# One hybrid decoder block on one core: where the HGRN mixer turns its keys and makes its states, how its scores share banks, and where the first attention maxima stand

## The chip, the cores and the metric

The kernel is one launch on 1 of the cores of a Trainium2 chip. The metric is the device time in microseconds (us) of that core. Before the change it is 3009.27 us, the median of 3 runs (3007.25 to 3016.14). The engines are named as in the profile: PE (TensorE, the matrix products), DVE (VectorE), ACT (ScalarE), POOL (GpSimd) and SP (SyncE, which issues most of the DMAs, one after the other).

## The reference: what is computed

One decoder block over a sequence of 2048 tokens of width 1024, in float32. One input projection feeds two mixers: HGRN2, a gated linear recurrence with 4 heads of 128, and a dilated attention with 8 heads of 64 and three branches (window, dilation) = (128,1), (512,4), (2048,16). An output projection and a SwiGLU follow, each with its norm, shift, scale, gate and residual.

```python
h = modulate(rms_norm(x, norm1_g[l]), shift1, scale1)
hq, hf, hi, hgt, aq, ak, av = jnp.split(h @ w_in[l], split_at, axis=-1)
...
def step(state, inp):                      # one chunk of the recurrence
    q_c, k_c, v_c, b_c = inp
    o_inter = jnp.einsum('bhtk,bhkv->bhtv', q_c * jnp.exp(b_c), state)
    ...
    scores = jnp.einsum('bhtk,bhsk,bhtsk->bhts', q_c, k_c, decay)
    o_intra = jnp.einsum('bhts,bhsv->bhtv', scores, v_c)
    k_dec = k_c * jnp.exp(b_last[:, :, None, :] - b_c)
    state = jnp.exp(b_last)[..., None] * state + jnp.einsum('bhsk,bhsv->bhkv', k_dec, v_c)
...
s_max = jnp.max(s, axis=-1, keepdims=True)  # attention: the maximum of each row of scores
p = jnp.exp(s - s_max)
```

## The kernel before

The tokens are taken in four pieces of 512 (`c` = 0 to 3); two pieces are a half. In each half the input projection makes all its columns tile by tile: a tile of `feature_major` is one block of 128 columns for 512 tokens, 24 matmuls of 128x512 (8 blocks of the depth, three products each, because every operand is split into a high and a low part; L565 to L567, or L463 to L465 for `token_major`). Their weights are loaded as `wraw`, rounded to `whi` on ACT (L87) and brought to the rest `wlo` on POOL (L80). A tile ends in `psA` (four banks of PSUM) and is moved out by ACT and DVE. PSUM has eight banks: four for `psA`, two for `psM`, one for `psL` and one for `psO`.

The HGRN mixer `hg_mix` is a generator that runs beside these projections. One run of it, called a unit here, is one head and one piece of 512 tokens (four chunks of 128); there are 16 units. A unit makes its gates with three exponentials and logarithms over 128x1536 on ACT (`he`), a running sum `hb` on DVE, and decayed keys `hkd`. Then, on PE:
- K, the keys turned: four transposes of `hkd` into `psM` (L620), copied by ACT to `hkt` (L622);
- U, the state products `u` = `hkt` times values into `psM` (L657); DVE makes the four new states `hst` from it (L666);
- seven levels of scores, s0 to s6. A level's operands `hz` are made by POOL (two differences `hd`), ACT (one exponential, L644) and DVE (two products); s0 has its own (`hzq`, and the `hz<-hk,hd` product). Each is four matmuls (L677) into `psL`, which DVE then copies under a mask into `hsc` (L682). `level(n)` makes the operands of level n; `level(n + 2)` follows the copy of level n;
- the outputs, into `psO` (L693, L694); the sum of their squares, called ss here (L701); and `hy`, which DVE makes from `psO` and writes to HBM as `hg_d`.

The generator's `yield`s cut a unit into steps. `Beside` hands out the steps: `begin(work, matmuls, steps, credit)` starts a list of units, and each time that `matmuls / steps` projection matmuls have been issued, one step follows; `finish` runs what is left. `UNIT` is 16, and two units are planned as 33 steps over 240 matmuls, 288 or 192. On PE the order is as written here (`manual_schedule`). On the other engines a scheduler of the compiler sets the order from the dependencies and its own estimate of times, once, when the program is built.

After the last unit `first_maxima` closes the pool of the mixer and opens that of the attention: `open_attention` issues loads of constants, queries and keys of head 0 (`qs`, `kh`), further operands (`qx`, `kl`) and values. Then `maxima_steps` makes the scores of 48 blocks two by two on PE (L133), and DVE takes their row maxima (L141), beside the last projection tiles `att_qk(1, 3)`. `combine` turns the maxima (L147), sends parts of them through HBM (`m_d`, `mr`, `mn_d`) and puts them into a row of `qx`. The attention follows: L896 and L898 are its scores, L856 its values, and the maxima of the next head run beside it into `psS`.

Of the kernel before, what the change touches and what calls it, by code (L numbers as in the profile page):

```python
# [11 lines left out]
F32 = mybir.dt.float32  # L12
# [38 lines left out]
def hybrid_block(ctx, tc, xT, small, cst, w_ada, w_ft, w_tk, w_out, w_gu, w_dn, out):  # L51
# [286 lines left out]
    with ExitStack() as ab:  # L338
# [129 lines left out]
        with tc.tile_pool(name="ada0", bufs=2) as pl:  # L468
            xs0 = []
            for k in range(KT):  # L470
                xs0.append(pl.tile([P, CH], F32, name=f"x0_{k}", bufs=1))
                nc.sync.dma_start(out=xs0[k], in_=xT[:, k, 0:CH])
            x_stats(0, xs0)
            h_tiles(0)
            ps0 = [pp.tile([P, CH], F32, name="psA", tag="psA", bufs=4) for _ in range(4)]
            tags = itertools.cycle(("psM", "psL"))

            def psum():
                tag = next(tags)
                return pp.tile([P, CH], F32, name=tag, tag=tag, bufs=2 if tag == "psM" else 1)  # L480

            LAG0 = 1

            bg = pl.tile([P, 8], F32, name="bg", bufs=1)
            dve.scalar_tensor_tensor(bg, sm[:, V_B + 8:V_B + 16], 1.0, sm[:, V_G1:V_G1 + 8], ALU.add, ALU.mult)
            sums, ws0 = {}, {}
            with tc.manual_schedule(engines={mybir.EngineType.PE}):
              done = {}
              for k in range(KT + LAG0):
                  if k < KT:  # L490
                      sums[k] = ada_sums(pl, cact, (k, 8 + k), 4, psum, 2)
                      if k % 2 == 0:
                          ws0[k] = ws0[k + 1] = split_w(wp, w_tk[0, k // 2])
                  if 0 < k <= KT:
                      n = k - 1
                      act.activation(mods[:, n:k], sums[n][:, 0:1], AF.Identity, bias=sm[:, V_B + n:V_B + k])
                      act.activation(gs1[:, n:k], sums[n][:, 1:2], AF.Identity, scale=sm[:, V_G1 + n:V_G1 + k],
                                     bias=bg[:, n:k])
                      with tc.issue_after(done[n - 2]) if n > 1 else nullcontext():
                          done[n] = h_apply(0, n, xs0[n])  # L500
                  if k >= LAG0:
                      token_major_k(0, k - LAG0, ps0, *ws0[k - LAG0])
# [90 lines left out]
        def hg_mix(hd, c, x):  # L593
# [21 lines left out]
            yield  # L615
            yield
            yield
            kt_ps = pp.tile([P, CH], F32, name="psM", tag="psM", bufs=2)
            for n in range(4):
                pe.transpose(kt_ps[:, n * P:(n + 1) * P], kd[:, n * P:(n + 1) * P], ident)  # L620
            kt = T("hkt")
            act.copy(kt, kt_ps)  # L622

            sc = T("hsc")
            lr = T("hd", 2)
# [20 lines left out]
                tt(dve, w(z)[:, :, 1, :], w(dd)[:, :, 1, :], w(q)[:, :, 1, :], ALU.mult)  # L646

            level(1)
            yield

            v = v_of[c]
            vn = [v[:, n, hd * P:(hd + 1) * P] for n in range(4)]
            ns = range(3 if c == NCH - 1 else 4)
            u = pp.tile([P, CH], F32, name="psM", tag="psM", bufs=2)
            for n in ns:
                ts = slice(n * P, (n + 1) * P)
                pe.matmul(u[:, ts], kt[:, ts], vn[n], start=n == 0, stop=n == ns[-1], skip_group_check=True)  # L657
            before = [states[hd]]
            for n in ns:
                ts = slice(n * P, (n + 1) * P)  # L660
                new = hw.tile([P, P], F32, name="hst", tag=f"hst{hd}", bufs=2) if n == 3 else \
                    hw.tile([P, P], F32, name="hst", tag="hst", bufs=3)
                if before[-1] is None:
                    dve.tensor_copy(new, u[:, ts])
                else:
                    dve.scalar_tensor_tensor(new, before[-1], eb[:, n * P + 127:n * P + 128], u[:, ts],  # L666
                                             ALU.mult, ALU.add)
                before.append(new)
            if len(ns) == 4:
                states[hd] = before[4]  # L670
            for lv in range(7):
                yield
                zk, zq = zs.pop(lv)
                ps = pp.tile([P, CH], F32, name="psL", tag="psL", bufs=1)
                for n in range(4):
                    ts = slice(n * P, (n + 1) * P)
                    pe.matmul(ps[:, ts], zk[:, ts], zq[:, ts], start=n == 0, stop=n == 3, skip_group_check=True)  # L677
                m = cs[:, C_MASK + lv * P:C_MASK + (lv + 1) * P].unsqueeze(1)
                if lv == 0:
                    tt(dve, c4(sc), c4(ps), m.broadcast_to([P, 4, P]), ALU.mult)  # L680
                else:
                    dve.copy_predicated(c4(sc), m.bitcast(U32).broadcast_to([P, 4, P]), c4(ps))  # L682
                if lv < 5:
                    level(lv + 2)
                elif lv == 5:
                    tt(dve, q, q, eb, ALU.mult)
            yield
            yield
            o_ps = pp.tile([P, CH], F32, name="psO", tag="psO", bufs=1)
            for n in range(4):  # L690
                ts = slice(n * P, (n + 1) * P)
                if before[n] is not None:
# [18 lines left out]
        def units(hd, xs):  # L711
            return [hg_mix(hd, c, x) for c, x in xs.items()]
# [42 lines left out]
        def second_half():  # L755
            token_major(1, 0)
            xs = hg_project(1, 0)
            for hd, others in ((1, lambda: att_qk(1, 0)), (2, lambda: token_major(1, 1, (2,))),
                               (3, lambda: token_major(1, 1, (3,)))):
                beside.begin(units(hd - 1, xs), 240, 2 * UNIT + 1)  # L760
                xs = hg_project(1, hd)
                others()
            beside.begin(units(3, xs), 192, 2 * UNIT + 1)
            att_qk(1, 1)
            att_qk(1, 2)
            beside.finish()

        first_psum = []

        def first_maxima():  # L770

            tags = itertools.cycle(("psL", "psO", "psM", "psM"))

            def psum():
                tag = next(tags)
                return pp.tile([P, CH], F32, name=tag, tag=tag, bufs=2 if tag == "psM" else 1)
            first_psum.append(psum)

            hwx.close()
            open_attention()  # L780
            beside.begin([maxima(0, psum)], 96 - 36, 24, -36)

        with tc.manual_schedule(engines={mybir.EngineType.PE}):
            make_h(1)
            first_half()
            make_h(2)
            make_h(3)
            second_half()
            first_maxima()
            att_qk(1, 3)  # L790
            beside.finish()
        combine(0, first_psum[0])
        dve.scalar_tensor_tensor(gs2, mods[:, 32:40], 1.0, sm[:, V_G2:V_G2 + 8], ALU.add, ALU.mult)


# [613 lines left out]
```

## Time and profile before

| what | value |
|---|---|
| median of 3 runs | 3009.27 us (3007.25 to 3016.14) |
| the profiled execution | 3006.01 us, span 3004.2 us |
| PE busy | 2829.4 us (94% of the span) |
| DVE, ACT, POOL busy | 68%, 44%, 47% |
| mean granted TensorE clock | 0.979 |

The units run from about 130 to 495 us (first half) and from 570 to 899 us (second half); the first maxima and the start of the attention lie between 899 and 966 us. After about 1215 us come the output projection and the SwiGLU. A view of the profile gives for each engine what it did and, in square brackets, how long it stood idle before an instruction and what ended that wait. The granted clock has two levels here, 1.0 (2.4 GHz) and 0.5 (1.2 GHz); a number between is a mean over a stretch.

### The profile page before, as it was taken

How to read it: one execution, taken by the hardware profiler on the slowest of the kernel's cores; microseconds unless marked ns; L12 is line 12 of the kernel's file. 1: busy time of each engine (PE TensorE's matmuls, PEld its weight loads, DVE VectorE, ACT ScalarE, POOL GpSimd, SP SyncE). 2: the span in 40 equal slices, each digit the busy share in tenths (PEclk: the TensorE clock that was granted, in tenths of full speed). 3: DMA queues.
4: the chain of work that ended last, by engine and by line, in shares of the span. 5: the costliest groups of instructions: out<-in, count | busy, mean ns of one | idle time of the engine just before them, and what ended most of it. 6: DMA issues, size and time to landing. Idle time of an engine off the chain costs nothing. (4 is left out here: it accounts for less than half of the span.)

```text
span 3004.2 us, 45023 instructions
## 1 busy us (share of the span) xinstructions
PE 2829.4 (94%) x16308; PEld 2601.9 (87%) x16308; DVE 2041.7 (68%) x3781; ACT 1313.2 (44%) x2392; POOL 1404.8 (47%) x1076
## 2 busy tenths in 40 slices
PE   6899999999997999999999999999999998999998
PEld 4777777787776999997778999999999998999998
DVE  7677756355554565677777676688677669776676
ACT  4533445344331665666554333345333335443334
POOL 5333443434332232320045666557566655665664
PEclk9999999999997999999999999999999999999999
DMA  6422335111138474537843222123242222232221
GB/s 245 151 99 103 111 141 180 62 64 69 55 116 210 120 164 104 134 109 251 294 158 130 82 73 85 64 78 108 83 133 74 81 71 93 85 114 65 84 75 66
DMA packets 212319, 344.37 MB, mean 115 GB/s; under 512 B 24816, under 2 KB 97392, under 8 KB 209008
## 3 DMA queue, kind: packets, MB, share of 16 engines
q1 hardware_dynamic: 202272, 323.40, 34.9%
q10 hardware_dynamic: 9824, 18.09, 1.6%
q8 instruction: 128, 2.10, 0.3%
q14 instruction: 95, 0.78, 0.1%
HBM read 282.44 MB, written 58.98 MB: 114 GB/s over the span
## 5 line engine op out<-in xcount | busy, mean ns | idle before, releaser
L80 POOL TENSOR_TENSOR wlo<-wraw,whi 128x512 fp32r<-128x512 f32 (+1 forms) x542 | 850.0, 1589 | 480.5 <-ACT whi L87 222.1
L1003 PE MATMUL psG<-chi,whi 128*128 128x344 f32 (+1 forms) x1848 | 596.4, 323 | 20.8 <-DVE hm L80 14.1
L1005 PE MATMUL psG<-chi,wlo 128*128 128x344 f32 (+1 forms) x1848 | 591.9, 320 | 1.5 <-POOL wlo L80 1.5
L1004 PE MATMUL psG<-clo,whi 128*128 128x344 f32 (+1 forms) x1848 | 593.2, 321 | 0.0
L274 ACT CAST whi<-wraw 128x512 fp32r<-128x512 f32 x520 | 311.0, 618 | 403.9 <-issue 191.6
L1003 PEld LDWEIGHTS psG<-chi,whi 128*128 128x128 f32 x1848 | 350.3, 190 | 26.5 <-DVE hm L80 9.3
L1265 PE MATMUL psD<-ahi,whi 128*128 128x344 f32 (+1 forms) x1056 | 346.5, 328 | 20.2 <-DVE xc L1268 19.7
L1268 DVE SCALAR_TENSOR_TENSOR xc<-psD,mods,xc 128x344 f32<-128x344 f32 (+1 forms) x528 | 290.2, 568 | 91.8 <-PE psD L1267 91.5
L1005 PEld LDWEIGHTS psG<-chi,wlo 128*128 128x128 f32 x1848 | 349.3, 189 | 2.7 <-POOL wlo L80 2.7
L1004 PEld LDWEIGHTS psG<-clo,whi 128*128 128x128 f32 x1848 | 349.1, 189 | 0.3 <-issue 0.2
L80 POOL TENSOR_TENSOR wlo<-wt,whi 128x512 fp32r<-128x512 f32 x132 | 192.6, 1469 | 314.6 <-ACT whi L274 238.3
L1267 PE MATMUL psD<-ahi,wlo 128*128 128x344 f32 (+1 forms) x1056 | 338.0, 320 | 0.0
L1266 PE MATMUL psD<-alo,whi 128*128 128x344 f32 (+1 forms) x1056 | 337.0, 319 | 0.0
L80 DVE TENSOR_TENSOR hm<-hm,psG 128x344 f32<-128x344 f32 (+1 forms) x330 | 165.8, 502 | 236.9 <-PE psG L1005 236.5
L565 PE MATMUL psA<-hhi,whi 128*128 128x512 f32 x640 | 272.1, 425 | 4.3 <-ACT hhi L417 2.6
L567 PE MATMUL psA<-hhi,wlo 128*128 128x512 f32 x640 | 253.9, 397 | 0.0
L566 PE MATMUL psA<-hlo,whi 128*128 128x512 f32 x640 | 253.0, 395 | 0.6 <-DVE hlo L80 0.6
L1265 PEld LDWEIGHTS psD<-ahi,whi 128*128 128x128 f32 x1056 | 199.4, 189 | 36.1 <-DVE xc L1268 31.7
L80 POOL TENSOR_TENSOR hd<-hb 128x256 f32<-128x256 f32 x192 | 130.7, 704 | 155.4 <-DVE hz L80 123.3
L1266 PEld LDWEIGHTS psD<-alo,whi 128*128 128x128 f32 x1056 | 199.6, 189 | 0.5
L1267 PEld LDWEIGHTS psD<-ahi,wlo 128*128 128x128 f32 x1056 | 199.5, 189 | 0.0
L274 ACT CAST whi<-wt 128x512 fp32r<-128x512 f32 x132 | 81.4, 616 | 235.0 <-DVE wt L80 139.4
(244 smaller groups left out, 5996.6 us busy)
## 6 DMA issues: line engine op xcount, KB each, us to landing
wraw<-in_w_gu SPq DMA_DIRECT2D x264, 256.0 KB, 2.9
wraw<-in_w_dn SPq DMA_DIRECT2D x132, 256.0 KB, 2.9
adaw<-in_w_ada SPq DMA_DIRECT2D x48, 512.0 KB, 4.8
wraw<-in_w_ft SPq DMA_DIRECT2D x42, 512.0 KB, 3.5
wraw<-in_w_tk SPq DMA_DIRECT2D x32, 512.0 KB, 3.5
qk_d<-st SPq DMA_DIRECT2D x64, 256.0 KB, 2.3
v<-v_d SPq DMA_DIRECT2D x16, 1024.0 KB, 6.1
wraw<-in_w_out SPq DMA_DIRECT2D x64, 256.0 KB, 3.6
```

The lines of the kernel that those rows point to most:

```text
L80: return eng.tensor_tensor(o, a, b, op)
L274: copy(hi, raw)
L565: pe.matmul(ps, whi[:, ws], hhi[:, k, :], start=k == 0, stop=False)
L566: pe.matmul(ps, whi[:, ws], hlo[:, k, :], start=False, stop=False)
L567: pe.matmul(ps, wlo[:, ws], hhi[:, k, :], start=False, stop=k == 7)
L1003: pe.matmul(ps, w[0][:, ws], hi, start=start and k == 0, stop=False, skip_group_check=True)
L1004: pe.matmul(ps, w[0][:, ws], lo, start=False, stop=False, skip_group_check=True)
L1005: last = pe.matmul(ps, w[1][:, ws], hi, start=False, stop=stop and k == 3, skip_group_check=True)
L1265: pe.matmul(ps, w[z][0][:, ws], ahi, start=z == 0, stop=False)
L1266: pe.matmul(ps, w[z][0][:, ws], alo, start=False, stop=False)
L1267: pe.matmul(ps, w[z][1][:, ws], ahi, start=False, stop=z == 1)
L1268: dve.scalar_tensor_tensor(x, ps, ga2[:, j:j + 1], x, ALU.mult, ALU.add)
```

## The change

Four edits go together:
- `psL` gets two banks, and `psO` is no longer a bank of its own: the outputs take a turn in the two banks of `psL`.
- K (the turning of the keys, now `turn()`) no longer stands ahead of the levels. It is a step of its own between level 0 and level 1. U and the states (now `state_updates()`) are a step of their own between level 2 and level 3. Level 0 follows one step after its operands are asked for. A unit has 16 steps in place of 15.
- The last two units of the second half run beside 144 projection matmuls in place of 192; `att_qk(1, 2)` is cut into its two pieces, and the second piece comes after `first_maxima()`. Its weights are loaded and split once more for that.
- The first maxima are spread over the 144 matmuls that are left, in place of 96, with another start and pace, and `combine(0)` is the last step of that list, ahead of the end of the projections, in place of behind them.

```diff
-                return pp.tile([P, CH], F32, name=tag, tag=tag, bufs=2 if tag == "psM" else 1)
+                return pp.tile([P, CH], F32, name=tag, tag=tag, bufs=2)
...
             yield
             yield
             yield
-            kt_ps = pp.tile([P, CH], F32, name="psM", tag="psM", bufs=2)
-            for n in range(4):
-                pe.transpose(kt_ps[:, n * P:(n + 1) * P], kd[:, n * P:(n + 1) * P], ident)
-            kt = T("hkt")
-            act.copy(kt, kt_ps)
...
             level(1)
-            yield
...
+            def turn():
+                kt_ps = pp.tile([P, CH], F32, name="psM", tag="psM", bufs=2)
...
+            def state_updates(kt):
...
             for lv in range(7):
+                if lv == 1:
+                    yield
+                    kt = turn()
+                elif lv == 3:
+                    yield
+                    before = state_updates(kt)
                 yield
                 zk, zq = zs.pop(lv)
-                ps = pp.tile([P, CH], F32, name="psL", tag="psL", bufs=1)
+                ps = pp.tile([P, CH], F32, name="psL", tag="psL", bufs=2)
...
-            o_ps = pp.tile([P, CH], F32, name="psO", tag="psO", bufs=1)
+            o_ps = pp.tile([P, CH], F32, name="psO", tag="psL", bufs=2)
...
-            beside.begin(units(3, xs), 192, 2 * UNIT + 1)
+            beside.begin(units(3, xs), 144, 2 * UNIT + 1)
             att_qk(1, 1)
-            att_qk(1, 2)
+            att_qk(1, 2, (2,))
             beside.finish()
...
-            tags = itertools.cycle(("psL", "psO", "psM", "psM"))
+            tags = itertools.cycle(("psL", "psM"))
...
-            beside.begin([maxima(0, psum)], 96 - 36, 24, -36)
+            beside.begin([maxima(0, psum), iter((combine(0, psum) for _ in range(1)))], 62, 24, -50)
...
             first_maxima()
+            att_qk(1, 2, (3,))
             att_qk(1, 3)
             beside.finish()
-        combine(0, first_psum[0])
```

**How instructions move.** On PE, in the last unit of the second half (`hkd` are the keys to be turned, `hkt` the turned ones, `hzq,hz` level 0, `hz` the later levels), before:

```order
L701 MATMUL psM<-hd,ones 128x512 [waits Activation_49]
...
L620 MATMUL psM<-cs,hkd 128x128 x4
...
L657 MATMUL psM<-vtok,hkt 128x128 [waits Activation_49]
L657 MATMUL psM<-vtok,hkt 128x128 x2
...
L677 MATMUL psL<-hzq,hz 128x128 [waits DVE_49,PE_49]
...
L677 MATMUL psL<-hz 128x128 [waits DVE_49]
```

and after:

```order
L713 MATMUL psM<-hd,ones 128x512 [waits Activation_49]
...
L689 MATMUL psL<-hzq,hz 128x128 [waits DVE_49,PE_49]
...
L650 MATMUL psM<-cs,hkd 128x128 [waits Pool_49]
...
L689 MATMUL psL<-hz 128x128 [waits DVE_49,PE_49]
...
L661 MATMUL psM<-vtok,hkt 128x128 [waits Activation_49]
L661 MATMUL psM<-vtok,hkt 128x128 x2
```

The rows left out are projection matmuls and the levels between. From K to U there were 6 projection matmuls in eight of the sixteen units and 9 in the others; now there are two levels and 21 projection matmuls (27 in the two units of the 288 stretch, 15 in the last two). From the ss of the first unit of a pair to level 0 of the second there were 42, and now there are 36 (54 and 45 in the 288 stretch, 33 and 21 in the last pair).

On SP, at the change to the attention (`qk_d<-st` are projection results on their way to HBM, `hg_d` the last unit's output, `kh<-qk_d` the keys that the first maxima need), before:

```order
L707 DMA hg_d_3_104<-hy 128x512
L575 DMA qk_d_0_84<-st 128x512
L576 DMA qk_d_1_85<-st 128x512
L170 DMA ca<-in_cst 128x256
L172 DMA idt<-in_cst 128x128
L174 DMA mtr<-in_cst 128x256
L213 DMA qs<-qk_d_0_72 64x2048
L213 DMA kh<-qk_d_0_80 64x2048
```

and after:

```order
L575 DMA qk_d_0_84<-st 128x512
L719 DMA hg_d_3_104<-hy 128x512
L576 DMA qk_d_1_85<-st 128x512
L575 DMA qk_d_0_76<-st 128x512
L170 DMA ca<-in_cst 128x256
L172 DMA idt<-in_cst 128x128
L174 DMA mtr<-in_cst 128x256
L213 DMA qs<-qk_d_0_72 64x2048
L213 DMA kh<-qk_d_0_80 64x2048
```

Before, the loads stand behind the last result of the tiles ahead of `first_maxima()`. After, one more row stands ahead of them, `qk_d_0_76<-st`: the result of the first tile behind `first_maxima()`.

On PE, at the start of the attention (`psT` are attention scores of head 0, `psS<-kh,qs` the maxima of head 1), before:

```order
L133 MATMUL psM<-kh,qs 128x128 x4
L147 MATMUL psL<-idt,mc 128x128
L896 MATMUL psT<-qs,kh 128x256 x3
L133 MATMUL psS<-kh,qs 128x128
L133 MATMUL psS<-kh,qs 128x256 x15
...
L133 MATMUL psS<-kh,qs 128x128 x16
L898 MATMUL psT<-qx_6873,kl_6874 128x256
```

and after:

```order
L147 MATMUL psL<-idt,mc 128x128
...
L567 MATMUL psA<-hhi,wlo 128x512
L905 MATMUL psT<-qs,kh 128x256 x3
L133 MATMUL psS<-kh,qs 128x128
L133 MATMUL psS<-kh,qs 128x256 x15
...
L133 MATMUL psS<-kh,qs 128x256 x3
L907 MATMUL psT<-qx_6813,kl_6814 128x256
```

Behind the last maxima of head 0 there are now 6 projection matmuls, L147 and 24 more projection matmuls. Of the 48 blocks of maxima of head 1, all stood ahead of the first L898; now 28 do, and 20 lie between the attention's later scores and values. From `first_maxima()` to the first maxima PE has 54 projection matmuls, where it had 39.

## Rows read from the trace of the kernel before

**Rows 1.** Windows: us, busy of each engine (instructions), granted clock, DMA share, GB/s.

```profile
130.00:495.00 365.00, 337.57 (x1777) 279.63 (x1775) 259.59 (x460) 152.48 (x210) 153.73 (x140) 0.99 0.35 120
570.00:899.00 329.00, 305.94 (x1608) 255.06 (x1607) 195.05 (x314) 130.42 (x179) 136.94 (x135) 0.97 0.20 72
791.00:795.00 4.00, 3.80 (x14) 3.22 (x15) 2.35 (x4) 1.72 (x3) 3.41 (x2) 0.60 0.00 0
948.00:964.00 16.00, 14.76 (x50) 12.30 (x51) 15.10 (x96) 0.00 (x0) 2.78 (x2) 0.50 0.92 225
```

**Rows 2.** Waits of PE, 68 to 1010 us: total us, times, longest.

```profile
PE psL L677 <- DVE hsc L682: 23.1, 20, 2.2
PE psM L657 <- ACT hkt L622: 18.8, 10, 3.6
PE psL L133 <- DMA kh<-qk_d: 8.1, 1, 8.1
PE psS L133 <- DMA mr<-m_d: 6.2, 1, 6.2
PE psA L463 <- DVE st L80: 3.6, 3, 2.2
...
PE psM L620 <- DVE hkd L80: 2.3, 1, 2.3
...
PE psM L620 <- issue: 1.8, 1, 1.8
```

**Rows 3.** Timeline at a wait for hsc: start, us, engine, line, operation [idle before <-releaser].

```profile
801.63 2.39 POOL L80 TENSOR_TENSOR wlo<-wraw,whi 128x1024 fp32r<-128x1024 f32 x1
...
801.93 2.37 DVE L80 TENSOR_TENSOR hz<-hd,hk 128x256 f32<-128x256 f32 x1
...
804.23 0.41 DVE L80 TENSOR_TENSOR hz<-hd,hq 128x256 f32<-128x256 f32 x1
...
807.08 0.70 DVE L682 COPY_PREDICATED hsc<-cs,psL 128x512 f32<-128x512 uint32 x1
...
807.84 1.16 PE L677 MATMUL psL<-hz 128*128 128x128 f32 x8 [2.22 <-DVE hsc L682]
```

**Rows 4.** Timeline at a wait for hkt.

```profile
789.19 1.48 ACT L599 ACTIVATE he<-he 128x1536 f32<-128x1536 f32 x1
790.58 0.57 ACT L622 COPY hkt<-psM 128x512 f32<-128x512 f32 x1
...
791.20 1.11 PE L657 MATMUL psM<-vtok,hkt 128*128 128x128 f32 x6 [1.98 <-ACT hkt L622]
```

**Rows 5.** Timeline of PE at full clock: two projections, and two levels.

```profile
796.54 0.40 PE L463 MATMUL psA<-whi,hhi 128*128 128x512 f32 x1
796.77 0.40 PE L464 MATMUL psA<-wlo,hhi 128*128 128x512 f32 x1
...
876.51 1.05 PE L677 MATMUL psL<-hz 128*128 128x128 f32 x8
...
878.79 1.05 PE L677 MATMUL psL<-hz 128*128 128x128 f32 x8
```

**Rows 6.** Timeline: ss of a unit, and the next unit's operand of level 0.

```profile
779.52 1.02 PE L701 MATMUL psM<-hd,ones 128*128 128x512 f32 x2
...
781.62 0.43 DVE L80 TENSOR_TENSOR hz<-hk,hd 128x256 f32<-128x256 f32 x1 [2.65 <-ACT hd L628]
```

**Rows 7.** Timeline at the first maxima: the tile boundary, SP's last key load, the wait.

```profile
899.01 0.39 PE L565 MATMUL psA<-hhi,whi 128*128 128x512 f32 x1
...
905.01 0.59 SPq L213 DMA_DIRECT2D kh<-qk_d  x1
...
916.14 0.77 PE L133 MATMUL psL<-kh,qs 128*128 128x128 f32 x2 [8.13 <-DMA kh<-qk_d]
```

**Rows 8.** Timeline at the start of the attention.

```profile
941.08 0.30 PE L147 MATMUL psL<-idt,mc 128*128 128x128 f32 x1 [0.66 <-issue]
...
942.34 0.46 SPq L213 DMA_DIRECT2D kh<-qk_d  x1
...
947.91 1.62 PE L133 MATMUL psS<-kh,qs 128*128 128x128 f32 x6 [6.18 <-DMA mr<-m_d]
```

More of the change, by code (lines that the diff above doesn't have):

```diff
@@ L648, in hg_mix @@
             level(1)
-            yield
             v = v_of[c]
             vn = [v[:, n, hd * P:(hd + 1) * P] for n in range(4)]
[L653 to L668, printed above, removed]
@@ L669, in hg_mix @@
-            if len(ns) == 4:
-                states[hd] = before[4]
-            for lv in range(7):
+            def turn():
+                kt_ps = pp.tile([P, CH], F32, name="psM", tag="psM", bufs=2)
+                for n in range(4):
+                    pe.transpose(kt_ps[:, n * P:(n + 1) * P], kd[:, n * P:(n + 1) * P], ident)
+                kt = T("hkt")
+                act.copy(kt, kt_ps)
+                return kt
+            def state_updates(kt):
+                ns = range(3 if c == NCH - 1 else 4)
+                u = pp.tile([P, CH], F32, name="psM", tag="psM", bufs=2)
+                for n in ns:
+                    ts = slice(n * P, (n + 1) * P)
+                    pe.matmul(u[:, ts], kt[:, ts], vn[n], start=n == 0, stop=n == ns[-1], skip_group_check=True)
+                before = [states[hd]]
+                for n in ns:
+                    ts = slice(n * P, (n + 1) * P)
+                    new = hw.tile([P, P], F32, name="hst", tag=f"hst{hd}", bufs=2) if n == 3 else \
+                        hw.tile([P, P], F32, name="hst", tag="hst", bufs=3)
+                    if before[-1] is None:
+                        dve.tensor_copy(new, u[:, ts])
+                    else:
+                        dve.scalar_tensor_tensor(new, before[-1], eb[:, n * P + 127:n * P + 128], u[:, ts],
+                                                 ALU.mult, ALU.add)
+                    before.append(new)
+                if len(ns) == 4:
+                    states[hd] = before[4]
+                return before
@@ L762, in second_half @@
                 others()
-            beside.begin(units(3, xs), 192, 2 * UNIT + 1)
+            beside.begin(units(3, xs), 144, 2 * UNIT + 1)
             att_qk(1, 1)
-            att_qk(1, 2)
+            att_qk(1, 2, (2,))
             beside.finish()
-        first_psum = []
         def first_maxima():
-            tags = itertools.cycle(("psL", "psO", "psM", "psM"))
+            tags = itertools.cycle(("psL", "psM"))
             def psum():
                 tag = next(tags)
-                return pp.tile([P, CH], F32, name=tag, tag=tag, bufs=2 if tag == "psM" else 1)
-            first_psum.append(psum)
+                return pp.tile([P, CH], F32, name=tag, tag=tag, bufs=2)
             hwx.close()
             open_attention()
-            beside.begin([maxima(0, psum)], 96 - 36, 24, -36)
+            beside.begin([maxima(0, psum), iter((combine(0, psum) for _ in range(1)))], 62, 24, -50)
         with tc.manual_schedule(engines={mybir.EngineType.PE}):
```

## The prediction

> **What bounds the kernel now.** Read the page's busy times first: PE is at work for most of the span, so a gain has to come out of the time in which PE stands still or runs at the lower clock. The windows by stage come next [rows 1]. In the two stretches with HGRN units PE is idle for 365.0 - 337.6 = 27.4 us and 329.0 - 305.9 = 23.1 us, 50.5 us together, while DVE is busy for 259.6 of 365 and 195.1 of 329 us: no other engine is full, so these gaps are waits for single results. The list of PE's waits names them [rows 2]: 23.1 us in 20 waits of scores (L677) for `hsc`, 18.8 us in 10 waits of U (L657) for `hkt`, 2.3 + 1.8 us of K (L620), and, outside the units, 8.1 us for the first key load and 6.2 us at the start of the attention. That is 60.3 us in the places that the change touches. Last comes the timeline at one wait of each sort.
>
> For `hsc` [rows 3]: the scores that start at 807.84 had waited 2.22 us for the copy of the level before, because there is one bank. The operands were not what was late: DVE finished a level's `hz` at 804.64 and then had other work (a running sum for the next unit) ahead of the copy at 807.08. For `hkt` [rows 4]: the copy on ACT starts at 790.58, behind the third of the next unit's three `he` operations, 1.48 us each; U waited 1.98 us for it.
>
> **The change part by part**, against the profiled execution's 3006.0 us (its span is 1.8 us shorter; the median of the runs lies 3.3 us above it).
>
> *Two banks for the scores, outputs among them.* A level now waits for the copy of two levels before, not of the last one. DVE makes a level's `hz` ahead of the copy that PE used to wait for [rows 3], so most of the 23.1 us goes. What is late next is the following `hz`: it stands behind the late copy. A level and six projections take 878.79 - 876.51 = 2.28 us, a projection 796.77 - 796.54 = 0.23 us [rows 5], so a group of scores takes about 0.90 us. A wait of up to 2.2 us is then cut, not wholly removed, where only six projections (1.4 us) follow; I put 3 us back. Term: -20.1 us. Bounds: -23.1 (nothing comes back) and -10 (more than half does). The output takes the bank until `hy` has read it; the next unit's level 1 needs it 36 projections and more (8.3 us) later, which hides that.
>
> *U behind two levels.* The longest wait was 3.6 us, behind 6 projections (1.4 us): the copy was at most 5.0 us behind K. Now 21 projections and two levels lie between, 21 x 0.23 + 2 x 0.90 = 6.6 us, and 15 and two levels, 5.25 us, in the last pair. I take -17.8 of the 18.8 us; bounds -18.8 and -9. The states are now late by three levels, but the outputs that read them come four levels after.
>
> *K one level later, level 0 one step sooner.* K's own waits (4.1 us) fall in the first unit of each half; there level 0 now arrives where the operands are just made. I take -3.1; bounds -4.1 and 0. In a second unit level 0 comes 36 projections, 8.3 us, after ss (4.8 us in the last). Its operand was ready at 781.62 + 0.43 = 782.05, 2.5 us after the ss at 779.52 [rows 6]. That hides it.
>
> *The clock.* After the wait of rows 4 the granted clock is 0.60 over 791 to 795 [rows 1]: a wait costs a second time, in projections at the lower level (1.2 GHz). Over the two stretches 0.99 and 0.97 are 365 x 0.01 + 329 x 0.03 = 13.5 us of full speed. Some of that goes with the waits; I take half, -7, with bounds -13.5 and 0.
>
> *The end of the projections.* Nothing of PE's work goes, 48 matmuls move behind `first_maxima()`. Three things change.
> - The first keys. PE passed the tile boundary at 899.01 and stood from 908.0; SP issued the last key load at 905.01, and it landed 11.1 us later [rows 7]. Now PE has 54 projections, 12.3 us, before it needs them. But SP holds the loads until the first tile behind the boundary (24 projections, 5.5 us) has been moved out, so the last load goes out at most 6.0 + 5.5 = 11.5 us after the boundary, where it was 6.0; I take 10.8, since only the first of that tile's two results stands ahead. It lands at 10.8 + 11.1 = 21.9: a wait of about 9.6 us in place of 8.1. Term +1.5; bounds -8.1 (the loads go out as early as before and land faster) and +4.
> - The start of the attention. There PE waited 6.18 us, while the last key load of head 1 went out at 942.34, after the final projection results, and landed with the end of the wait [rows 8]. Now it stands on SP ahead of those results, and PE has 24 projections (5.5 us) after L147. Term -5.2; bounds -6.2 and 0.
> - The maxima of head 1. From 948 to 964 DVE is busy for 15.1 of 16 us at 48 of them, 0.315 us each, with PE at clock 0.50 [rows 1]: DVE is the bound there. 20 of the 48 move into the attention, where PE pays for them; a PE group costs no more there than DVE's 0.315. Bounds -6.3 and 0, and I take the middle, -3.
>
> Sum of this part: -6.7 us. The second loading of two weight tiles adds two casts on ACT and two differences on POOL of 2.39 us each [rows 3], and two DMAs on SP. They have a tile of 24 projections (5.5 us) to hide behind, and about 1.0 + 2.39 us to do (the cast is an estimate: two thirds of the 1.48 us of a `he` operation [rows 4], which has one and a half times its columns). What else grows is PE's wait for DVE to empty `psA`, 3.6 us now [rows 2], since PE comes sooner. Together +4 us; bounds 0 and +10.
>
> One rule speaks against this. In rows 3 a product `hz` that takes 0.41 us took 2.37 us beside a `wlo` on POOL of 2.39 us, and both end within 0.3 us. The Trainium skill, page "SBUF — State Buffer", section "SBUF: two separate sides", says that a VectorE operation with two SBUF inputs and a GpSimd operation that reads SBUF exclude each other for the whole instruction. By that rule, which the row agrees with, the two added differences could hold DVE for 2 x 2.0 = 4.0 us more, and the sum would be 4 us higher if PE waited for all of it.
>
> Sum: -20.1 - 17.8 - 3.1 - 7 - 6.7 + 4 = -50.7 us, so 2955.3 on the profiled execution and 2958.6 on the median. I take 2957.
>
> **The rivals.**
> - *The last part gives nothing.* The key loads stand behind one more projection result, and SP does nothing out of its order. If the first wait grows by 4 us and the other two terms are nothing: -44 + 4 = -40, 2966. For it: the order on SP. Against it: 24 projections now cover the second wait.
> - *Half comes back.* PE arrives sooner, and the operands `hz` or `hkt` are then what is late, since POOL, ACT and DVE still do the same work in a shorter time: half of the first two terms (-19), -1.5 for K, half of the last part (-3.3), no clock, +4: -20, 2986. For it: the 2.37 us product [rows 3]. Against it: DVE is idle for over a quarter of these stretches [rows 1].
> - *It gives all that it could.* -23.1 - 18.8 - 4.1 - 13.5 - 12.5 = -72, 2934.
> - *Nothing to be seen.* Nearly all the waits return under another name, -5: 3001. It needs engines that are full, which rows 1 do not show.
> - *Slower.* ACT's three `he` operations of the next unit, 3 x 1.48 = 4.4 us [rows 4], used to hold only `hkt`. Now K's copy comes two levels later, and they could fall ahead of the exponential that a level's `hz` needs; then PE waits in each of the 16 units, 71 us in all, and the sum is +20: 3026. It decides from 50.7 / 16 = 3.2 us a unit. Against it: `he` of the next unit is not tied to K, and an `hz` is made a level ahead.
>
> **How the numbers follow.** Chances: the forecast 0.53 (2940 to 2975), the last part for nothing 0.13, half back 0.15, all of it 0.07, nothing to be seen 0.06, slower 0.06. About 0.3%, 9 us, is what a measurement can tell here. Faster by more than that: the first four less 0.02 for the upper end of half back, 0.86. Within it: 0.08. Slower: 0.06. The range is 2934 to 2992: from the full gain to a little above half back. It leaves out the last two cases and the edges of the others, some 0.2.
>
> **What would show it.** In the profile after: the waits of scores for `hsc` under 4 us and of U for `hkt` under 2 us; waits of scores for `hz` under 6 us in all; a clock of 0.99 in both stretches; a wait of 7 to 11 us at the first maxima, still; under 2 us at the first maxima of head 1. It is wrong if scores wait for `hz` for more than 15 us in all, if the wait at the first keys is gone (then the order on SP did not matter), or if PE waits for `psA` for more than 10 us.

## The result, and the profile after

The changed kernel takes 2968.38 us (median of 4 runs, 2966.09 to 2973.43), the kernel before 3009.11 beside it on the same chip: a ratio of 0.9867 with a 95% interval of 0.9854 to 0.9879, or 40 us less (36 to 44). The forecast was 2957 with a range of 2934 to 2992. The profiled execution took 2968.5 us with a span of 2966.7, 37.5 us less than the span before. Executions of one kernel differ by up to some 14 us, and the longer ones mostly show a lower mean granted clock, so a difference of a few us between two kernels stays open.

First the windows, with the columns of [rows 1]: the two stretches with HGRN units, and then the stretch from the 96th projection matmul to the 2400th, which holds fourteen of the sixteen units.

```profile
130.00:490.00 360.00, 335.42 (x1785) 282.36 (x1784) 265.57 (x463) 153.60 (x212) 155.34 (x140) 0.99 0.36 124
560.00:870.00 310.00, 302.80 (x1632) 255.61 (x1632) 200.49 (x315) 132.59 (x180) 148.18 (x139) 0.99 0.24 81
69.50:801.00 731.50, 694.06 (x3566) 580.30 (x3566) 489.50 (x802) 309.73 (x421) 308.88 (x262) 0.99 0.32 110
```

And the same pair of matmuls in the kernel before:

```profile
68.90:828.90 760.00, 705.89 (x3565) 582.64 (x3563) 480.32 (x805) 313.38 (x424) 307.96 (x265) 0.98 0.31 105
```

The fourteen units became 760.0 - 731.5 = 28.5 us shorter. PE's idle time fell from 54.1 to 37.4 us, by 16.7; its busy time for the same matmuls fell by 11.8 us, at a mean granted clock of 0.99 in place of 0.98. The last two units stand beside the next 192 projection matmuls. First the kernel before, then the changed one:

```profile
828.90:899.01 70.11, 65.41 (x362) 54.99 (x363) 39.67 (x70) 23.97 (x39) 25.83 (x28) 1.00 0.32 115
```

```profile
801.00:871.08 70.08, 66.93 (x364) 56.22 (x363) 45.63 (x73) 28.11 (x44) 35.14 (x34) 0.98 0.39 133
```

There PE's idle time fell from 4.7 to 3.2 us, but the stretch is no shorter. What follows it took 2095.6 us where it had taken 2105.2, 9.6 us less. (The first 96 matmuls end 0.6 us later.) The two stretches show unequal halves: PE is idle for 24.6 of 360 us in the first (27.4 of 365 before) and for 7.2 of 310 in the second (23.1 of 329).

The waits of PE from 68 to 1010 us, in the columns of [rows 2]:

```profile
PE psL L689 <- DVE hz L80: 21.7, 16, 3.0
PE psL L133 <- DMA kh<-qk_d: 10.3, 1, 10.3
PE psA L565 <- DVE st L80: 5.3, 2, 4.1
PE psA L463 <- DVE st L80: 4.2, 2, 3.3
...
PE psA L464 <- POOL wlo L80: 2.4, 1, 2.4
```

The waits for `hsc` (23.1 us), `hkt` (18.8) and K's (4.1) are gone, all of them. In their place the scores wait for `hz`: 21.7 us in 16 waits; the list before has no wait for `hz`. 16.7 of the 21.7 us stand at level 5, in ten of the sixteen units. One of them, in the timeline, with DVE's queue and what POOL did beside it:

```profile
198.93 1.05 PE L689 MATMUL psL<-hz 128*128 128x128 f32 x8
...
199.54 1.30 POOL L80 TENSOR_TENSOR hd<-hb 128x256 f32<-128x256 f32 x2 [1.72 <-DVE hz L80]
...
200.88 1.23 DVE L607 TENSOR_TENSOR_SCAN hb<-rst,hlf 128x512 f32<-128x512 f32 x1 [1.08 <-POOL hd L80]
...
202.02 1.47 DVE L670 SCALAR_TENSOR_TENSOR hst<-hst,heb,psM 128x128 f32<-128x128 f32 x4
...
204.45 0.69 DVE L80 TENSOR_TENSOR st<-psA,st 128x512 fp32r<-128x512 f32 x1 [0.96 <-ACT st L519]
...
205.06 0.71 DVE L694 COPY_PREDICATED hsc<-cs,psL 128x512 f32<-128x512 uint32 x1
205.67 0.41 DVE L80 TENSOR_TENSOR hz<-hd,hk 128x256 f32<-128x256 f32 x1
...
206.56 0.77 PE L689 MATMUL psL<-hz 128*128 128x128 f32 x2 [2.94 <-DVE hz L80]
```

The scores of level 3 end at 199.98, so their copy could start there, and `hz` of level 5 behind it. DVE gets to that copy 5.1 us later. Ahead of it in its queue stand the next unit's running sum `hb`, held 1.08 us until POOL has read the old `hb`, the four state updates, and an evacuation of `psA` held 0.96 us for ACT. For two of these five microseconds DVE stands still, each time behind the one instruction that is next in its queue.

At the change to the attention: SP's row of the first tile, its last load, the first maxima, and the first maxima of head 1 [rows 7, 8].

```profile
864.70 0.38 SPq L719 DMA_DIRECT2D hg_d<-hy  x1
...
867.22 0.32 SPq L575 DMA_DIRECT2D qk_d<-st  x1
867.59 0.45 SPq L170 DMA_DIRECT2D ca<-in_cst  x1
...
870.95 0.61 SPq L213 DMA_DIRECT2D kh<-qk_d  x1
...
882.93 0.77 PE L133 MATMUL psL<-kh,qs 128*128 128x128 f32 x2 [10.33 <-DMA kh<-qk_d]
...
916.58 0.97 PE L133 MATMUL psS<-kh,qs 128*128 128x128 f32 x6 [1.05 <-DVE st L80]
```

The first wait is 10.33 us (8.13 before), the last load lands 12 us after its issue, and the wait at the attention's start is 1.05 us (6.18 before).

### The profile page after: what moved, and what is told of

Same layout as the page of the kernel before. It is cut to its first block, busy times and chain, and to the rows that moved or that the text cites. A ratio compares the mean times of both kernels' runs of the same rounds, so it can differ in the third digit from the quotient of the medians.

```text
span 2966.7 us, 45106 instructions
## 1 busy us (share of the span) xinstructions
PE 2815.3 (95%) x16308; PEld 2598.6 (88%) x16308; DVE 2054.9 (69%) x3781; ACT 1313.6 (44%) x2394; POOL 1414.7 (48%) x1078
## 5 line engine op out<-in xcount | busy, mean ns | idle before, releaser
L1012 PE MATMUL psG<-chi,whi 128*128 128x344 f32 (+1 forms) x1848 | 596.3, 323 | 20.3 <-DVE hm L80 12.9
```

What stands on the lines that cost most here:

```text
L1012: pe.matmul(ps, w[0][:, ws], hi, start=start and k == 0, stop=False, skip_group_check=True)
```

## The experiments

Each kernel was timed beside the kernel before, and "us" from a ratio is of 3008. Experiments 1 to 3 are one part alone, 9 and 12 two parts.

**1. Two banks alone.**

```diff
-tag=tag, bufs=2 if tag == "psM" else 1)     # both lists of banks
+tag=tag, bufs=2)
-name="psL", tag="psL", bufs=1)
+name="psL", tag="psL", bufs=2)
-name="psO", tag="psO", bufs=1)
+name="psO", tag="psL", bufs=2)
```

> The kernel before with two banks for the scores and the outputs in them; keys, states and the end as before. Theory A (a wait for DVE follows behind the bank: hsc was one late result, and hz stands behind it on DVE): the 23.1 us for hsc go, 8 to 12 us come back as waits for hz, the hkt waits stay near 18.8 us, so the time falls by 10 to 16 us, to about 2996. Rival B (my predicted size): hz waits near 3 us, the time falls by 20 us or more, to 2989 or less. Rival C (the bank only passes the wait on): less than 5 us.

Measured: 2989.02 us, ratio 0.9930 (0.9917 to 0.9942), 21 us less (17 to 25). Its waits:

```profile
PE psM L657 <- ACT hkt L622: 18.8, 10, 3.6
...
PE psL L677 <- DVE hz L80: 8.2, 9, 1.9
```

Theory A's waits with rival B's time: `hsc` is gone, 8.2 us return as `hz`. The time gains more than these 14.9 us: in the fourteen units PE's idle time fell by 12.1 us (54.1 to 42.0), and its busy time for the same matmuls by 9.8 (705.9 to 696.1).

**2. Keys and states moved, alone.** The changed kernel with `psL` of one bank, `psO` of its own, and the end as before.

> The changed kernel with one bank for the scores, one of its own for the outputs, and the end of the projections as before: only the keys turned later and the states made later. Theory A: the waits for hkt (18.8 us) and hkd (2.3 us) go, the waits for hsc stay at 20 us or grow to 30, because the four state updates now stand on DVE between two copies hsc; the time falls by 8 to 18 us. Rival B (independent terms as predicted): hsc waits stay at 23, the time falls by 18 to 21 us. Rival C: hsc waits grow by all that hkt gave, and the time is the same within 5 us.

Measured: 3007.84 us, ratio 0.9999 (0.9990 to 1.0008): nothing. Its waits, and the units' window:

```profile
PE psL L689 <- DVE hsc L694: 41.6, 23, 3.7
...
PE psL L689 <- DVE hsc L80: 3.5, 4, 1.2
```

```profile
70.30:835.80 765.50, 706.99 (x3565) 586.35 (x3564) 486.36 (x801) 310.31 (x420) 308.70 (x262) 0.97 0.30 104
```

Rival C: `hkt` and K are gone, and the waits for `hsc` rose from 23.1 to 45.1 us, by 22.0, as much as `hkt` and K had held (22.9). The fourteen units are 5.5 us longer in this profile, whose execution is one of the longer ones (3012.6 us); they are not shorter.

Where the waits stand tells why. 28.1 of the 45.1 us are at level 4, in fifteen of the sixteen units; before, level 4 had 12.1 us in ten. One of them:

```profile
737.67 1.23 DVE L607 TENSOR_TENSOR_SCAN hb<-rst,hlf 128x512 f32<-128x512 f32 x1 [1.68 <-POOL hd L80]
...
738.82 1.09 DVE L670 SCALAR_TENSOR_TENSOR hst<-hst,heb,psM 128x128 f32<-128x128 f32 x3
...
739.82 0.72 DVE L694 COPY_PREDICATED hsc<-cs,psL 128x512 f32<-128x512 uint32 x1
...
740.60 1.16 PE L689 MATMUL psL<-hz 128*128 128x128 f32 x8 [1.70 <-DVE hsc L694]
```

The copy of level 3 stands on DVE behind the held scan, as it did before, and now also behind the state updates, which U has brought there. So part of the 22.0 us is the place to which U moved its updates, as theory A had said, and not only that PE comes sooner. How much is which was not measured.

**3. The end alone.** The kernel before with the last 48 projection matmuls behind `first_maxima()`, and the lists of the change.

> The kernel before with the end of the projections of the changed one (48 projection matmuls behind the first key loads, maxima sooner, combine in the list), the units as before. Theory A (the end is independent of the units, as aligned by projection matmuls, 10.5 us): the time falls by 8 to 13 us, the wait at the first keys is 8 to 12 us, the one at the first maxima of head 1 under 2 us. Rival B (the predicted size): 5 to 8 us. Rival C (what the end gives is a cover for units that come sooner): under 4 us.

Measured: 3008.44 us, ratio 1.0004 (0.9995 to 1.0013): nothing, rival C. Waits from 830 us on:

```profile
PE psA L565 <- ACT whi L87: 5.5, 1, 5.5
PE psL L133 <- DMA kh<-qk_d: 5.0, 1, 5.0
PE psL L677 <- DVE hsc L682: 3.9, 2, 2.0
```

The 6.2 us at the attention's start are gone as intended. But 5.0 us stand at the keys and 5.5 at the weights of the fourth tile behind `first_maxima()`, 10.5 us together, as much as the changed kernel has at the keys alone. (The load of these weights goes out at 915.13, behind the key loads and a projection result at which SP stands for 13.4 us; in the changed kernel it went out at 863.80, ahead of them.) And PE waits 3.9 us for `hsc` and 1.3 for `hkt` in the last two units, at 144 matmuls in place of 192, where it had waited 0.6 and 4.1.

**9. Banks with keys and states, without the end.**

> The changed kernel with the end of the projections as before: two banks and the moved keys and states together, without the third part. The parts alone gave 19.4 us (banks), 0.6 (keys and states) and nothing (the end), 20 us together, where all three give 39 to 40. Theory A (two banks and the moved keys need each other: alone, the moved keys turn the hkt waits into hsc waits, 23.1 to 45.1 us): this kernel gives 28 to 36 us against the kernel before, and the end 4 to 10 us behind it. Rival B (it is the end that needs the two banks, since its last unit's levels stand closer): this kernel gives 19 to 24 us, the end the rest. The waits for hz are 18 to 24 us by A and 8 to 12 by B.

Measured: 2982.71 us, ratio 0.9911 (0.9898 to 0.9925), 27 us less (23 to 31). Waits:

```profile
PE psL L689 <- DVE hz L80: 18.9, 15, 3.0
```

Theory A's waits, and nearly its time. The moved keys, worth nothing alone, are worth some 6 us beside two banks (the intervals of the two kernels overlap, but their fourteen units agree with it, 731.9 us here and 738.1 in experiment 1), and `hz` goes from 8.2 to 18.9 us. Up to the 2400th projection matmul this profile and the changed kernel's are as one (27.6 and 27.9 us ahead of before). By the runs the end is then worth 13 us, by the profiles 2.4: the profiled execution took 2970.9 us, and the other four took 10 to 14 us more. The record shows a mean granted clock of 0.982 for the profiled one and of 0.978 or 0.979 for these four, where the changed kernel's four have 0.982 to 0.984. An estimate from these clocks, 0.0035 x 2980, is some 10 us, so most of the 13 us goes with the clock. That the end raises the clock is not shown.

**12. Banks with the end, keys and states as before.**

> The kernel before with two banks and the changed end of the projections; keys and states as before. Known: banks alone 19.4 us, the end alone nothing, banks with keys and states 27 us, all three 40. Theory A (the end's quicker last unit needs two banks, or it waits for hsc): this kernel gives 28 to 34 us, the end 9 to 14 of it. Rival B (the end needs the shorter units of the moved keys: it still waits for hkt in its last units): 18 to 23 us, nothing from the end. The hkt waits stay near 16 to 20 us in both; by A the waits in the last unit are no longer than in the banks alone, by B some 5 us longer.

Measured: 2982.01 us, ratio 0.9932 (0.9918 to 0.9945), 20 us less (17 to 25): by the ratio no more than the banks alone. Waits from 830 us on:

```profile
PE psA L565 <- ACT whi L87: 5.0, 1, 5.0
PE psL L133 <- DMA kh<-qk_d: 4.8, 1, 4.8
```

Rival B's time. Its mechanism isn't there: `hkt` costs nothing in the last two units. By the spans of the profiled executions the end is worth 8.5 us here (2988.2 to 2979.7), by the ratios nothing; in experiment 9 the spans gave 2.4 and the runs 13. The profiles show two sides of the end. From the 2400th projection matmul to the last one it makes the kernel longer, by 8.7 us in experiment 3, 6.5 here and 4.2 in the changed kernel (against the kernel before, experiment 1 and experiment 9); behind the last one it makes it shorter, by 9.1, 14.5 and 6.3 us.

**4. State updates behind level 5.** `elif lv == 3` before `state_updates(kt)` becomes `elif lv == 6`.

> The changed kernel with U and its four state updates behind level 5 instead of behind level 2. Theory A (the four updates on DVE, 1.47 us in a row with other work, make hz late): the waits of the scores for hz fall from 21.7 to 8 to 14 us, new waits of the outputs for hst are under 5 us, and the time falls by 4 to 10 us against the changed kernel (2968 to 2958 to 2964). Rival B (hz is late through its chain over GpSimd and ACT, or because PE comes sooner): hz waits stay at 18 or more, the time moves by less than 4 us. Rival C: the states are then late for the outputs, and the time grows by 5 us or more.

Measured: 2979.92 us, ratio 0.9903 (0.9889 to 0.9916), 11 us slower than the changed kernel.

```profile
PE psL L689 <- DVE hz L80: 27.1, 20, 2.6
```

Theory A fell. With the updates gone from there, level 5 still waits 18.6 us, behind the scan `hb`, and level 3 waits 5.7 us more. Rival C has the time, though not its reason: the outputs wait for no `hst`.

**5. Without most of the modulation sums.** Only the first `adaacc` operation of each pair is left.

> The changed kernel without seven of the eight operations by which DVE sums each pair of modulation columns beside the first half's projections (adaacc; 16 pairs, 112 operations of 0.47 us, some 53 us of DVE). This leaves part of the modulation sums out. Theory A (in the first half DVE's queue makes hz and the emptying of psA late): the waits for hz in the first half fall from 14.7 us to 5 to 9 (the second half, which has no such work, has 7.0), the waits for psA there from some 12 to under 5, and the time falls by 10 to 20 us to 2948 to 2958. Rival B (hz is late through its own chain): hz waits in the first half stay above 12, the time falls by less than 5 us.

Measured: 2958.12 us, ratio 0.9841 (0.9828 to 0.9854), 8 us under the changed kernel, with intervals that just touch. First-half waits (68 to 560 us; 14.7 us for `hz` in the changed kernel), and the units' window:

```profile
PE psL L689 <- DVE hz L80: 6.5, 5, 1.7
PE psA L565 <- DVE st L80: 5.0, 2, 3.9
PE psA L463 <- DVE st L80: 4.2, 2, 3.3
```

```profile
69.60:785.00 715.40, 688.67 (x3566) 575.24 (x3565) 434.93 (x690) 310.19 (x420) 305.02 (x262) 1.00 0.33 112
```

Theory A for `hz`, though the time falls by less than its 10 us: 54.6 us less of DVE (489.5 to 434.9) take 8.2 us of its waits away, and the fourteen units are 16.1 us shorter. For `psA` it fell: those waits stayed as they were, so they are not made by `adaacc`.

**6. Half of the modulation sums moved to the second half.** The pairs from 32 on start behind `hg_project(1, 0)`, spread over 900 matmuls.

> The changed kernel with the second eight of the sixteen pairs of modulation sums moved from the first half's projections to the second half's. DVE is busy for 266 of 360 us in the first half's stretch and for some 200 of 310 in the second's; 56 operations of 0.47 us, 26 us, move over. Theory A (DVE's queue): the first half's hz and psA waits fall by about half, 10 to 13 us, the second half's grow by 3 to 6; the time falls by 4 to 10 us to 2958 to 2964. Rival B (the waits follow the work): as much comes back in the second half, within 4 us of 2968.

Measured: 2970.91 us, ratio 0.9882 (0.9866 to 0.9897): not told apart from the changed kernel. In the second half (560 to 870 us):

```profile
PE psL L689 <- DVE hz L80: 8.8, 8, 2.3
PE psO L706 <- DVE hsc L694: 4.3, 2, 2.2
```

Rival B. The first half's `hz` fell from 14.7 to 10.0 us; the second half gained 1.8 for `hz` (from 7.0) and 4.3 for the outputs: 6.1 back for 4.7. (All of the first half's waits together fell by 3.1 us, from 33.3 to 30.2, since others came up there.)

**10. Two buffers for `hb`.**

```diff
-T("hlf"), T("hb"), T("heb")
+T("hlf"), T("hb", 2), T("heb")
-name="adaacc", tag="adaacc", bufs=2)
+name="adaacc", tag="adaacc", bufs=1)
```

> The changed kernel with two buffers for the running sum hb (and, to make room, one buffer in place of two for adaacc). 16.7 of the 21.7 us of hz waits stand at level 5, in 10 of the 16 units; there DVE has the next unit's scan into hb (1.23 us, held until GpSimd has read the old hb for level 6) and the four state updates in a row ahead of that level's hz. Theory A (the scan held by its one buffer): the scan moves ahead, the waits at level 5 fall from 16.7 to 4 to 9 us, the time by 5 to 10 us against the changed kernel. Rival B (the four updates alone suffice): level 5 keeps 13 us or more, the time moves by less than 4 us. Rival C (the scan ahead delays the levels 2 and 3 by as much): the waits move to other levels, and their sum stays within 4 us of 21.7.

Measured: 2964.92 us, ratio 0.9852 (0.9838 to 0.9865): the lowest of the kernels that compute all, but not told apart from the changed one. `hz`, 21.7 before:

```profile
PE psL L689 <- DVE hz L80: 17.6, 13, 2.8
```

Level 5 fell from 16.7 to 10.9 us, and levels 3 and 4 have 2.8 in place of 0.6. The held scan is a part of the cause, about a third of level 5 and a fifth of the whole; the rest keeps its place behind the state updates. The buffer taken from `adaacc` is a second edit, which was not tried alone.

**11. Three buffers for `hz`.** `T("hz", 2)` becomes `T("hz", 3)` in both places, with one buffer for `adaacc`.

> The changed kernel with three buffers for the level operands hz in place of two (and one for adaacc in place of two). With two, DVE can make a level's hz only after the scores of two levels before, behind whatever has come between; with three it stands a level sooner, and the scan and the state updates fall behind the hz of level 5. Theory A (the two buffers make hz late): the waits of scores for hz fall from 21.7 to under 8 us, the time by 8 to 15 us against the changed kernel, to 2953 to 2960. Rival B (DVE's total work sets the pace, whatever its order): the waits return for hsc, hst or psA, and the time moves by less than 4 us. Rival C (hd's two buffers on GpSimd and ACT hold hz instead): hz waits stay above 15 us.

Measured: 2975.77 us, ratio 0.9891 (0.9877 to 0.9904), about 7 us slower than the changed kernel, with intervals that just overlap.

```profile
PE psL L689 <- DVE hsc L694: 21.3, 22, 3.3
...
PE psL L689 <- DVE hz L80: 0.7, 1, 0.7
```

```profile
70.50:812.60 742.10, 700.51 (x3565) 582.12 (x3565) 486.75 (x802) 310.14 (x420) 310.96 (x262) 0.98 0.32 108
```

Rival B for the waits, to the microsecond, though the time moved by more than its 4 us: `hz` is made a level sooner and is hardly ever late, and the same 21 us return for `hsc`. PE's idle time in the fourteen units is 41.6 us (37.4 in the changed kernel).

**7. Head 0's loads in two halves.** `dst[:, cut]` and `src[a, cut]` for the first 1024 columns of all four, then for the others.

> The changed kernel with head 0's four key and query loads cut into two halves of 1024 columns, the first halves ahead of the second. Theory A (the wait at the first keys is the time in which four loads of 512 KB land, 12 us behind the last issue, and the first maxima need only the first columns): the wait of 10.3 us falls to 3 to 6 us, and the time by 3 to 7 us. Rival B (the order on SP sets it; cutting only adds four issues of 0.6 us): the wait stays at 9 to 12 us, the time within 3 us.

Measured: 2971.82 us, ratio 0.9887 (0.9874 to 0.9901): no gain (6 us more than the changed kernel by the ratios, with intervals that just overlap).

```profile
PE psS L133 <- DMA kh<-qk_d: 7.2, 1, 7.2
...
PE psL L133 <- DMA kh<-qk_d: 4.9, 1, 4.9
```

The wait at the first maxima is theory A's, 4.9 us in place of 10.3: half of it goes with the second halves of the four loads. In the time there is nothing of theory A. The 5.4 us come back as 7.2 us at head 1's first maxima: the last of head 1's loads goes out 39.9 us behind the first four (876.53 to 916.43), where it was 38.5 (870.95 to 909.47), while PE is there sooner.

**8. The first tile's rows on ACT's queue.** `att_qk(1, 2, (3,))` issues its results by `nc.scalar`.

> The changed kernel with the results of the one tile pair behind first_maxima() issued by ACT's queue instead of SP's, so that no result of a later tile stands ahead of the key loads on SP. Theory A (SP is held by that result): in the changed kernel SP stood 1.6 us at it (865.63 to 867.22); the loads go out 1.5 to 2 us sooner and the wait falls from 10.3 to 8 to 9 us, the time by 1 to 2 us. Rival B (the loads wait for the boundary itself, the last unit's output): no change. Rival C (the held SP was the whole of it, as the prediction's bound of -8.1 has it): the wait falls by 5 us or more.

Measured: 2972.26 us, ratio 0.9891 (0.9875 to 0.9908): no gain (7 us more by the ratios, with intervals that just overlap).

```profile
873.46 0.38 SPq L719 DMA_DIRECT2D hg_d<-hy  x1
...
874.44 0.78 SPq L170 DMA_DIRECT2D ca<-in_cst  x1
...
879.82 0.45 SPq L213 DMA_DIRECT2D kh<-qk_d  x1
...
890.76 0.77 PE L133 MATMUL psL<-kh,qs 128*128 128x128 f32 x2 [9.45 <-DMA kh<-qk_d]
```

From the last unit's output to `ca` SP now needs 0.98 us, not 2.89; but to the last load 6.36 us, where it was 6.25. With nothing held ahead of them the issues of the constants and loads spread out; why is not shown. The row on SP was not what made the loads late.

## Why the prediction was nearly right

It was right in direction and within its range. For the waits that the change was to remove, its mechanism was right too; the way it added them was not. That the total came out within the range is in part luck. Over the sixteen units PE's idle time fell by 18.2 us (16.7 and 1.5), where -37 had been forecast with the +4 in it; the clock and what follows the units gave some 5.6 us more than forecast and hid a part of that.

- *Two banks, -20.1.* By the waits they gave 14.9 us (23.1 for `hsc` gone, 8.2 for `hz` come), within the bounds of -23.1 and -10. That the time fell by 21 us (experiment 1) agrees with the term by luck: it holds the 9.8 us of busy time, and the forecast has the clock as a term of its own.
- *U behind two levels, -17.8, and K, -3.1.* Both waits vanished, as worked out, but they were worth nothing with one bank (experiment 2) and some 6 us with two (9 against 1). The failed step is the sum of these terms. It took them for independent, since each had its own row. With the waits for `hkt` gone, the scores stood for 22.0 us more at the next thing that DVE owed: PE came sooner, and the state updates had moved to just ahead of it. That "the states are now late by three levels" was weighed for the outputs, which read them, and not for the copies and products that stand behind them on DVE.
- *What is late next, 3 us of `hz`.* The place was named (the following `hz`, behind the late copy); the size was 21.7 us. It was taken from one wait's pattern before, with DVE's queue as it stood when PE waited longer. This is the term that moved the forecast: its 18.7 us are as much as the 18.8 by which PE's idle time in the sixteen units missed (-37 forecast, -18.2 measured). By the prediction's own test, over 15 us, the step is wrong.
- *The clock, -7.* About right. The stretches show 0.99 and 0.99, where 0.99 and 0.97 stood; by the forecast's own working that leaves (360 + 310) x 0.01 = 6.7 of the 13.5 us, so 6.8 went. PE's busy time for the same matmuls in the fourteen units fell by 11.8 us, but profiles 7 and 8, with the same units, show 8.2 and 5.2.
- *The first keys, +1.5.* The wait was forecast at 9.6 us and is 10.33. That SP's order makes it is not borne out: experiment 8 takes the row away, and the last load goes out no sooner. The bytes of the loads make about half of it: with half of them in the first four loads, these landed 6.5 us behind the last issue, not 12 (7).
- *The attention's start, -5.2.* 6.18 to 1.05 us, as forecast. The maxima of head 1 (-3) were not measured apart. All that follows the units gives 9.6 us in the profile against 6.7 for this part, with whatever the clock does there. But alone, beside the banks and beside both other parts the end is worth 0, 0 and 13 us by the ratios (experiments 3, 12, 9) and 0, 8.5 and 2.4 by the profiles; what it needs for its gain stays open.
- *Added waits, +4.* The waits for `psA` on `st`, `wlo` and `vtok` grew from 7.5 to 12.9, all of them in the first half. (The 3.6 us of the forecast is one row of these. All waits for `psA` were 10.7 us before and are 15.9 now, so its test of 10 us was passed before the change.) The two added differences on POOL are the ones at 849.86 and 861.37, beside the last unit. (Counted from the last: the two behind them, at 866.78 and 874.06, belong to the tiles of `att_qk(1, 3)`, as the last two before did.) The first held a product `hz` for 2.60 us, which takes 0.42 alone, and PE waited 0.96 us for it:

```profile
849.86 2.48 POOL L80 TENSOR_TENSOR wlo<-wraw,whi 128x1024 fp32r<-128x1024 f32 x1 [1.68 <-ACT whi L87]
850.03 2.60 DVE L80 TENSOR_TENSOR hz<-hd,hq 128x256 f32<-128x256 f32 x1
...
852.77 1.13 PE L689 MATMUL psL<-hz 128*128 128x128 f32 x8 [0.96 <-DVE hz L80]
```

The rule of the Trainium skill, page "SBUF — State Buffer", section "SBUF: two separate sides", is about a VectorE operation with two SBUF inputs and a GpSimd operation that reads SBUF. The rows agree: `hz` reads two tiles in SBUF and ends 0.29 us behind the difference. Beside the second difference (861.37 to 863.78) `st`, which reads one of its two inputs from `psA`, takes its usual 0.68 us, and `hy<-hy,hgs`, which reads two tiles in SBUF, 1.20 us in place of 0.69. Of the 4.0 us that the forecast had for this, DVE was held for some 2.7, and 0.96 reached PE.

Of the rivals, "half comes back" was the truest picture of the units (`hz` late since PE comes sooner), and the clock and the end made good for it. "DVE is idle for over a quarter", which was held against it, didn't help: experiments 4, 6 and 11 change what DVE does first and when, and 22 to 27 us of waits of the scores and outputs stay. Only less work on DVE (5), or an operation that no longer holds its queue (10), lowered them; of the two, only experiment 5 can be told apart from the changed kernel in time, and barely.

## What to carry to other kernels

Two waits of one engine are not two terms of a sum: a wait that is removed alone can return in full under another name, at the next result that is owed. So for each removed wait ask what the serving engine still has queued ahead of the next result, with the work that the change itself puts there, and judge it with the earlier arrival; an average idle share of a quarter doesn't cover bursts of 5 us in a queue whose order is fixed. Try parts in pairs as well as alone: here two parts that were each worth nothing stood, by the runs, for half of the whole gain. And compare the granted clock of the executions before a difference of some 10 us is laid to an edit.

## What the runs showed that was not expected

- The clock moves by as much as a term. In the fourteen units the same matmuls took 705.9 us of PE before, 694.1 after, and 688.7 in experiment 5, at 0.98, 0.99 and 1.00. But experiments 7 and 8, whose units are those of the changed kernel with the same waits (22.0 us for `hz`), show 697.7 and 700.7 us at 0.98. So a part of the 11.8 us is a difference between executions.
- DVE was held by POOL more often than before. Of the 224 operations that write `hz`, 25 took over 1 us, each of them beside a POOL operation; before it was 14. They cost DVE some 46 us over their usual time, where it had been some 25. Four of the sixteen waits for `hz`, 3.1 us, stand right behind such a one; what the others owe to it was not measured.
- A `hkt` wait and a `hsc` wait trade nearly one for one (22.9 gone, 22.0 come), and so do `hz` and `hsc` (21.0 and 21.3).
- Loads that can be issued sooner need not be: without the held row, SP took 5.38 us from `ca` to the last `kh`, where it had taken 3.36.
